# First MLP matrix on one Trainium2 core: upper and lower weight parts in fours, with a second copy of the input

## The chip, the cores and the metric

The program runs on one core of one Trainium2 chip. A core has TensorE (matrix products), VectorE, ScalarE, GpSimd and SyncE, which issues most of the transfers; in the profile they are PE (and PEld for its weight loads), DVE, ACT, POOL and SP. The metric is the device time of one execution in microseconds; lower is better. The kernel before takes 2034.71 us, the median of 3 runs (2034.69 to 2035.07).

## The reference

The reference is a small trunk of two layers over 256 tokens of width 2048 (all float32). Layer 0 mixes tokens with a convolution module, layer 1 with a latent attention; each is followed by an MLP with a squared ReLU. The MLP is what matters here:

```python
def sq_relu_mlp(h, w1, w2):
    return jnp.square(jax.nn.relu(h @ w1)) @ w2

# per layer: h is the RMS-normed input (256 x 2048),
# w1 is 2048 x 8192, w2 is 8192 x 2048
x = x + sq_relu_mlp(h, mlp_w1[layer], mlp_w2[layer])
```

## The kernel before

**Two parts per number.** The products keep float32 accuracy with a cheaper operand type (float32r). Every operand is split in an upper part, the value rounded to float32r, and a lower part, what is left. A product a x b is then three: upper x upper, upper x lower and lower x upper. ScalarE makes the upper part of the weights (`split_half`, L154, tile `hi`) and VectorE the lower part (L155, tile `lo`), from a raw tile that SyncE's queue loads from HBM (L144). There are three raw tiles, and six tiles each of `hi` and `lo`; one of these holds two k, a k being 128 rows of the weights.

**The input of the MLP.** The tokens are normed, transposed by TensorE (`to_T`, L237) and written as four tiles `xt`, each 128 x 4 x 512: for each k the upper part of 256 tokens (ScalarE, L186) and beside it the lower part of the same 256 tokens (VectorE, L193). `xhl(k)` is the whole 512 columns, `xh(k)` the first 256 alone. The transposes go through two PSUM buffers (`tr`). This happens block by block in `prepare`, while the product before (the last product of the convolution module or of the attention) still runs; the last block follows its end.

**The product with the first MLP matrix** (`mlp`, L397 and L398). The 8192 columns are taken in two halves of 8 groups of 512 columns. A group has four sums of 128 weight columns each, in four of the six PSUM buffers `acc`. For each of the 16 k, and each of the four sums, TensorE does two products. L397 takes the upper part of the weights as stationary operand and streams all 512 columns of `xhl(k)`; so upper x upper lands in the first half of the sum and upper x lower in the second half. L398 takes the lower part of the weights and streams the 256 columns of `xh(k)` into the first half. The order is L397, L398, L397, L398 and so on. At the end of a group ScalarE copies the second half out (L405), VectorE adds the first (L406), squares the positive part (L407), and both make the upper and lower parts `gh` and `gl` (L409, L410).

**The product with the second MLP matrix** (`product_A`, with `mm3` at L180 to L182) follows after each half. There `gh` and `gl` are stationary and the weights are streamed, 512 columns at a time, in the order `gh` x `hi`, `gl` x `hi`, `gh` x `lo`. `mm3` also serves the last products of the convolution module and of the attention, and the attention's input product, where `xt` is the stationary operand.

**What sets the order.** The convolution and attention stages have an order written out by hand. The MLP stages and the products around them are ordered by the framework's scheduler, which places instructions by its own costs; each engine then runs its list in order. Waits are semaphores between the lists.

**Where tiles lie.** Pools are stacked from both ends of the on-chip memory, and small pads (`PAD_CONST`, `PAD_SMALL`, `PAD_RIGHT`, `PAD_KV`, `PAD_O`) shift what follows. By the addresses of the built program `hi`, `lo`, `gh` and `gl` begin at multiples of 64 bytes, and `xt` begins 32 bytes off a multiple of 64. The first set of `xt` serves the convolution, the MLP of layer 0 and the attention's input; the second set is opened ahead of the MLP of layer 1.

Of the kernel before, what the change touches and what calls it, by code (L numbers as in the profile page):

```python
# [10 lines left out]
F32 = mybir.dt.float32  # L11
F32R = mybir.dt.float32r
# [6 lines left out]
P = 128  # L19
D = 2048  # L20
KC = D // P
T = 2
S = T * P
FF = 4 * D
NB = 512
NNB = D // NB
# [11 lines left out]
PAD_SMALL = 48  # L38
PAD_RIGHT = 48
PAD_KV = 40  # L40
PAD_O = 56
WB = 6
LOOK = WB // 2 - 1
# [29 lines left out]
def trunk_kernel(  # L73
# [26 lines left out]
    nc = tc.nc  # L100
# [8 lines left out]
    def repool(name, **banks):  # L109

        psum_cx[0].close()
        psum_cx[0] = ExitStack()
        for kind, n in banks.items():
            psum[kind] = psum_cx[0].enter_context(tc.tile_pool(name=kind + name, bufs=n, space=PSUM, reuse_waits="tile"))
# [13 lines left out]
    def nm(s):  # L128
        uid[0] += 1
        return f"{s}_{uid[0]}"  # L130
# [5 lines left out]
    def tr_tile():  # L136
        return psum["tr"].tile([P, NB], F32, tag="tr", name=nm("tr"))
# [46 lines left out]
    def hi_part(ps, hi, scale=1.0):  # L184

        nc.scalar.activation(hi, ps, AF.Copy, scale=scale)  # L186

    def lo_part(ps, hi, lo, scale=None):

        if scale is None:  # L190
            nc.vector.tensor_tensor(lo, ps, hi.bitcast(F32), op=ALU.subtract)
        else:
            nc.vector.scalar_tensor_tensor(  # L193
                out=lo, in0=ps, scalar=scale, in1=hi.bitcast(F32), op0=ALU.mult, op1=ALU.subtract
            )
# [33 lines left out]
            nc.vector.tensor_scalar(ms, ssq[:, :, 0], scalar1=1.0 / dim, scalar2=None, op0=ALU.mult)  # L229
        return rsqrt(ms, T, EPS, name)  # L230

    def to_T(src, k0, hi, lo, gain, pt=None):

        pt = pt if pt is not None else tr_tile()
        for j in range(2):
            for t in range(T):
                nc.tensor.transpose(  # L237
                    pt[:, j * S + t * P : j * S + (t + 1) * P],
                    src[:, t, (k0 + j) * P : (k0 + j + 1) * P],
                    ident,  # L240
                )
        ps = [pt[:, j * S : (j + 1) * S] for j in range(2)]
        for j in range(2):
            hi_part(ps[j], hi(k0 + j), gain[:, k0 + j : k0 + j + 1])
        for j in range(2):
            lo_part(ps[j], hi(k0 + j), lo(k0 + j), gain[:, k0 + j : k0 + j + 1])

    repool("c", acc=4, tr=2, sum=2)


    xs = main.tile([P, T, D], F32, name="xs")
# [31 lines left out]
    g_mlp = [vecs[:, 2 * KC : 3 * KC], vecs[:, 3 * KC : 4 * KC]]  # L283
# [1 line left out]
    b_dw = vecs[:, 6 * KC : 7 * KC]  # L285


    xt_cx, xt = [ExitStack()], []

    def right_pool(name, bufs):  # L290

# [3 lines left out]

    ctx.callback(lambda: xt_cx[0].close())

    def open_xt(name):
        pool = right_pool(name, 1)
        xt[:] = [  # L300
            pool.tile([P, KC // NNB, 2 * S], F32R, name=nm("xt")) for _ in range(NNB)
        ]

    xhl = lambda k: xt[k // 4][:, k % 4, :]
    xh = lambda k: xhl(k)[:, :S]
    xl = lambda k: xhl(k)[:, S:]
    open_xt("xt0")
    scratch = main.tile([P, NB], F32, name="scratch")

    xh_kt = lambda k, t: xh(k)[:, t * P : (t + 1) * P]  # L310
    xl_kt = lambda k, t: xl(k)[:, t * P : (t + 1) * P]

    def residual_stage(last, gain, r_scale=None):


        ssq = small.tile([P, T, NNB], F32, tag="ssq", name=nm("ssq")) if last else None

        def add(n, ps, t):
            sl = slice(n * NB, (n + 1) * NB)
            if r_scale is None:  # L320
                nc.vector.tensor_tensor(xs[:, t, sl], ps[t], xs[:, t, sl], op=ALU.add)
            else:
                nc.vector.scalar_tensor_tensor(
                    out=xs[:, t, sl], in0=ps[t], scalar=r_scale[:, t : t + 1], in1=xs[:, t, sl],
                    op0=ALU.mult, op1=ALU.add,
                )

        def prepare(n, only=None):
            sl = slice(n * NB, (n + 1) * NB)
            if last:  # L330
                if gain is not None:
                    for j in range(2):
                        to_T(xs, 4 * n + 2 * j, xh, xl, gain)
                for t in range(T) if only is None else [only]:
                    nc.scalar.activation(scratch, xs[:, t, sl], AF.Square, accum_out=ssq[:, t, n : n + 1])

        return ssq, add, prepare
# [39 lines left out]
    def mlp(layer, ssq, next_gain, finish=None):  # L377

        with ExitStack() as cx:
            mp = cx.enter_context(tc.tile_pool(name=f"mp{layer}", bufs=1, reuse_waits="tile"))  # L380
            nkh = FF // P // HALVES
            r2 = small.tile([P, T], F32, tag="r2", name=nm("r2"))
            nssq = None
            for hf in range(HALVES):
                hh, hl = [], []
                for g in range(nkh // 4):
                    ps = [acc_tile() for _ in range(4)]
                    c0 = (hf * nkh + 4 * g) * P
                    for u in range(KC // 4):
                        wj = load_split([rows(mlp_w1[layer], 4 * u, 4, c0, NB)], 4)  # L390
                        for j in range(4):
                            k = 4 * u + j
                            wh, wl = wj(j)
                            for b in range(4):
                                bs = slice(b * P, (b + 1) * P)

                                nc.tensor.matmul(ps[b], wh[:, bs], xhl(k), start=k == 0, stop=False)  # L397
                                nc.tensor.matmul(ps[b][:, :S], wl[:, bs], xh(k), start=False, stop=k == KC - 1)  # L398
                    gh = mp.tile([P, 4, S], F32R, tag="gh", name=nm("gh"), bufs=nkh // 4)
                    gl = mp.tile([P, 4, S], F32R, tag="gl", name=nm("gl"), bufs=nkh // 4)  # L400
                    for b2 in range(2):
                        v = mp.tile([P, 2, S], F32, tag="v", name=nm("v"), bufs=2)
                        for b in range(2):
                            o = ps[2 * b2 + b]
                            nc.scalar.activation(v[:, b, :], o[:, S:], AF.Copy)  # L405
                            nc.vector.tensor_tensor(v[:, b, :], o[:, :S], v[:, b, :], op=ALU.add)  # L406
                        nc.vector.scalar_tensor_tensor(out=v, in0=v, scalar=0.0, in1=v, op0=ALU.max, op1=ALU.mult)  # L407
                        bs = slice(2 * b2, 2 * b2 + 2)
                        nc.scalar.activation(gh[:, bs, :], v, AF.Copy)  # L409
                        nc.vector.tensor_tensor(gl[:, bs, :], v, gh[:, bs, :].bitcast(F32), op=ALU.subtract)  # L410
                    hh.append(gh)
                    hl.append(gl)
                if hf == 0:
                    r = rms_rstd(ssq, NNB, D, "n")
                    nc.vector.tensor_tensor(r2, r, r, op=ALU.mult)
                nssq, add, prepare = residual_stage(hf == HALVES - 1, next_gain, r2)
                product_A(
                    mlp_w2[layer],
                    hf * nkh,
                    nkh,  # L420
                    lambda k, t: hh[k // 4][:, k % 4, t * P : (t + 1) * P],
                    lambda k, t: hl[k // 4][:, k % 4, t * P : (t + 1) * P],
                    add,
                    prepare,
                    finish=(lambda t: finish(nssq, t)) if finish is not None and hf == HALVES - 1 else None,
                )
            return nssq


    with ExitStack() as cx:  # L430
# [172 lines left out]
        with tc.manual_schedule():  # L603
# [57 lines left out]
            for c in range(1, KC + 1):  # L661
                n = UC * c
# [81 lines left out]
            for m in range(NP):  # L744
# [4 lines left out]
                for j in range(2):  # L749
                    k = 2 * m + j  # L750
                    wh, wl = conv_w(NU + m, j)
                    for b in range(2):
                        bs = slice(b * NB, (b + 1) * NB)
# [2 lines left out]
                conv_split(NU + m + 2)  # L756
                conv_load(NU + m + 5)

        ssq, add, prepare = residual_stage(True, g_mlp[0])
        for b in range(2):  # L760
            for t in range(T):
                add(b, ps2[b], t)
# [58 lines left out]
    ssq = mlp(0, ssq, g_mix[1])  # L821


    with ExitStack() as cx:
# [98 lines left out]

        pad_kv = at.tile([P, PAD_KV], F32, name="pad_kv")
        nc.gpsimd.memset(pad_kv, 0.0)  # L925
# [4 lines left out]
        kpT = at.tile([P, S], F32, name="kpT")  # L930
        pad_o = at.tile([P, PAD_O], F32, name="pad_o")
        nc.gpsimd.memset(pad_o, 0.0)
# [168 lines left out]
        with tc.manual_schedule():  # L1101
# [8 lines left out]
            ps = [[acc_tile() for _ in range(2)] for _ in range(T)]  # L1110
            for k in range(KC):
                u, j = divmod(k, 2)
# [4 lines left out]
                wh, wl = w_at(("kv", u), j)  # L1117
# [9 lines left out]
            ps = [acc_tile() for _ in range(T)]  # L1127
            for k in range(KC):
                u, j = divmod(k, 4)
# [3 lines left out]
                wh, wl = w_at(("q", u), j)  # L1133
# [16 lines left out]
                if k == 13:  # L1150
                    pt = tr_tile()
# [31 lines left out]
            for g in range(NG):  # L1183
                for i in range(HG):
                    h = g * HG + i

                    n = -(-len(work) // (HG - i))
# [18 lines left out]
                o_piece(k)  # L1206
            prefetch()

        open_xt("xt1")
        ssq, add, prepare = residual_stage(True, g_mlp[1])  # L1210
        for b in range(2):
            for t in range(T):
                add(b, ps_o[b], t)
# [47 lines left out]
```

## Time and profile before

| | us |
|---|---|
| time, median of 3 runs | 2034.71 |
| the profiled execution's own time | 2034.44 |
| its span, first to last instruction | 2032.6 |
| TensorE busy | 2009.5 |
| VectorE busy | 1214.8 |
| ScalarE busy | 951.7 |
| GpSimd busy | 174.2 |
| granted TensorE clock, mean | 0.999 of full |
| memory traffic over the span | 180 GB/s |

In time order: the convolution module up to about 336 us, the first MLP (L397 first starts at 336.2), the attention between the MLPs, and the second MLP up to the end (L397 last starts at 1848.5; its second product follows).

How to read it: a row of the page's groups gives the line, the engine, the operation, output and inputs by tile names, the shape, the count, then busy time and the mean duration of one; the last column is the idle time of the engine ahead of them. The durations of TensorE's products overlap: a product's record includes the time until its last result is out, while the next one has already begun. So the distance between two starts, in the timeline, is the time that a product costs in a stream. Starts in the timeline are rounded to 0.01 us; a distance is therefore read over many products.

### The profile page before, as it was taken

What the parts mean: (1) busy time and instruction counts of PE and PEld (TensorE: products, weight loads), DVE (VectorE), ACT (ScalarE), POOL (GpSimd) and SP (SyncE); (2) the same over time, 40 slices, a digit from 0 to 9 for tenths busy, and PEclk for the clock granted to TensorE, in tenths of its full rate; (3) what the DMA queues carried; (4) which work ended last, traced back from release to release, by engine and by line L of the source; (5) the groups of instructions that cost most, each with busy time, mean ns of one, the idle gap of its engine ahead of it and who ended that gap; (6) DMA issues with size and microseconds to landing.
All of it is one profiled execution on the core that took longest, in us unless ns stands there. A gap on an engine that the chain in (4) does not pass through costs nothing.

```text
span 2032.6 us, 27882 instructions
## 1 busy us (share of the span) xinstructions
PE 2009.5 (99%) x11132; PEld 1747.1 (86%) x11132; DVE 1214.8 (60%) x1820; ACT 951.7 (47%) x1325; POOL 174.2 (9%) x101
## 2 busy tenths in 40 slices
PE   7999999999999999999999999999999999999998
PEld 7999888888888888888899887888888888888886
DVE  5999866665544465555446654665564455565454
ACT  5444655544433454444445444554443334454442
POOL 5887400000000000000000000000000000000000
PEclk9999999999999999999999999999999999999999
DMA  7555355665555665555555344566655566655552
GB/s 235 166 167 166 125 186 180 194 187 188 202 189 190 196 193 187 187 193 193 187 162 170 108 139 145 187 207 187 188 196 196 188 196 192 192 187 189 199 192 104
DMA packets 243268, 367.59 MB, mean 181 GB/s; under 512 B 15417, under 2 KB 89793, under 8 KB 242881
## 3 DMA queue, kind: packets, MB, share of 16 engines
q1 hardware_dynamic: 242400, 364.68, 56.0%
q8 instruction: 87, 1.43, 0.3%
q10 hardware_dynamic: 736, 1.12, 0.2%
q14 instruction: 45, 0.36, 0.0%
HBM read 363.68 MB, written 2.10 MB: 180 GB/s over the span
## 4 chain that ended last, share of the span: by engine, by line
PE 98%; DVE 1%; DMA 0%; ACT 0%; issue 0%; SPq 0%; DVEq 0%; ACTq 0%
PE acc L397 23%; PE acc L180 16%; PE acc L182 16%; PE acc L181 16%; PE acc L398 12%; PE acc L482 3%; PE acc L484 3%; PE acc L483 3%; PE sum L515 1%; PE acc L1049 1%; PE tr L237 1%; PE acc L1048 1%; PE acc L971 0%; PE acc L994 0%; PE acc L972 0%; PE acc L973 0%
## 5 line engine op out<-in xcount | busy, mean ns | idle before, releaser
L155 DVE TENSOR_TENSOR lo<-raw,hi 128x1024 fp32r<-128x1024 f32 (+1 forms) x628 | 755.2, 1206 | 685.1 <-ACT hi L154 673.3
L154 ACT ACTIVATE hi<-raw 128x1024 fp32r<-128x1024 f32 (+1 forms) x696 | 722.4, 1046 | 792.0 <-PE acc L181 458.3
L397 PE MATMUL acc<-xt,hi 128*128 128x512 f32 x2048 | 710.5, 390 | 0.0
L398 PE MATMUL acc<-xt,lo 128*128 128x256 f32 x2048 | 577.7, 282 | 0.0
L397 PEld LDWEIGHTS acc<-xt,hi 128*128 128x128 f32 x2048 | 384.4, 188 | 80.5
L180 PE MATMUL acc<-hi,gh 128*128 128x512 f32 x1024 | 398.6, 389 | 0.0
L182 PE MATMUL acc<-lo,gh 128*128 128x512 f32 x1024 | 398.4, 389 | 0.0
L181 PE MATMUL acc<-hi,gl 128*128 128x512 f32 x1024 | 398.4, 389 | 0.0
L398 PEld LDWEIGHTS acc<-xt,lo 128*128 128x128 f32 x2048 | 387.1, 189 | 0.1
L182 PEld LDWEIGHTS acc<-lo,gh 128*128 128x128 f32 x1024 | 192.2, 188 | 40.1
L180 PEld LDWEIGHTS acc<-hi,gh 128*128 128x128 f32 x1024 | 192.2, 188 | 39.7
L181 PEld LDWEIGHTS acc<-hi,gl 128*128 128x128 f32 x1024 | 192.2, 188 | 39.6
L549 DVE SCALAR_TENSOR_TENSOR sum<-ub,w_dw,sum 128x256 f32<-128x256 f32 x402 | 167.7, 485 | 4.9 <-ACT sum L518 2.9
L155 POOL TENSOR_TENSOR lo<-raw,hi 128x1024 fp32r<-128x1024 f32 x68 | 162.1, 2407 | 57.2 <-ACT hi L154 57.2
L482 PE MATMUL acc<-xt,hi 128*128 128x256 f32 x512 | 147.3, 288 | 0.0
L484 PE MATMUL acc<-xt,lo 128*128 128x256 f32 x512 | 143.2, 280 | 0.6 <-POOL lo L155 0.6
L483 PE MATMUL acc<-xt,hi 128*128 128x256 f32 x512 | 143.1, 279 | 0.0
L484 PEld LDWEIGHTS acc<-xt,lo 128*128 128x128 f32 x512 | 96.2, 188 | 0.8 <-POOL lo L155 0.8
L483 PEld LDWEIGHTS acc<-xt,hi 128*128 128x128 f32 x512 | 96.3, 188 | 0.6 <-DVE xt L193 0.2
L482 PEld LDWEIGHTS acc<-xt,hi 128*128 128x128 f32 x512 | 96.3, 188 | 0.4
L925 POOL MEMSET pad_kv<- 128x40 f32 x1 | 0.1, 132 | 772.6 <-PE acc L182 772.6
L405 ACT ACTIVATE v<-acc 128x256 f32<-128x256 f32 x128 | 46.4, 381 | 25.3 <-PE acc L398 25.3
(200 smaller groups left out, 1718.6 us busy)
## 6 DMA issues: line engine op xcount, KB each, us to landing
raw<-in_mlp_w SPq DMA_DIRECT2D x256, 1024.0 KB, 5.2
raw<-in_conv_w_pw SPq DMA_DIRECT2D x64, 512.0 KB, 4.9
raw<-in_conv_w_pw SPq DMA_DIRECT2D x16, 1024.0 KB, 5.1
raw<-in_mla_w_o SPq DMA_DIRECT2D x16, 1024.0 KB, 5.7
raw<-in_mla_w_kv_up SPq DMA_DIRECT2D x8, 1024.0 KB, 5.3
raw<-in_mla_w_in SPq DMA_DIRECT2D x8, 576.0 KB, 3.7
raw<-in_mla_w_in SPq DMA_DIRECT2D x4, 1024.0 KB, 5.0
raw<-in_mla_w_q_up SPq DMA_DIRECT2D x16, 256.0 KB, 3.2
```

What stands on the lines that cost most here:

```text
L154: nc.scalar.activation(hi, raw[:, js, :], AF.Copy)
L155: eng.tensor_tensor(lo, raw[:, js, :], hi.bitcast(F32), op=ALU.subtract)
L180: nc.tensor.matmul(ps, sh, mh, start=start, stop=False)
L181: nc.tensor.matmul(ps, sl, mh, start=False, stop=False)
L182: nc.tensor.matmul(ps, sh, ml, start=False, stop=stop)
L397: nc.tensor.matmul(ps[b], wh[:, bs], xhl(k), start=k == 0, stop=False)
L398: nc.tensor.matmul(ps[b][:, :S], wl[:, bs], xh(k), start=False, stop=k == KC - 1)
L405: nc.scalar.activation(v[:, b, :], o[:, S:], AF.Copy)
L482: nc.tensor.matmul(o, wh[:, bs], xh(k), start=k == 0, stop=False)
L483: nc.tensor.matmul(o, wh[:, bs], xl(k), start=False, stop=False)
L484: nc.tensor.matmul(o, wl[:, bs], xh(k), start=False, stop=k == KC - 1)
L549: nc.vector.scalar_tensor_tensor(out=out, in0=ubs[c][:, w : w + S], scalar=tap(c, w), in1=pcs[c], op0=ALU.mult, op1=ALU.add)
```

## The change

The four upper-part products of a k are done first, then the four lower-part products. The lower-part products no longer stream `xh(k)`, the first half of `xt`, but `xh2(k)`, a second copy of the upper part of the input in its own four tiles `xu` (128 x 4 x 256). ScalarE writes this copy from the same PSUM buffer as the first, behind the lower part, in `to_T`; 16 more activations for each MLP. A pad of 8 floats lies between `xt` and `xu`. The pool with both is opened ahead of each MLP's input, so the convolution's `xt0` keeps its place and layer 0's MLP gets a set of its own (`xt1`; layer 1's becomes `xt2`). By the addresses of the built program `xt1` and `xt2` begin at multiples of 64 bytes and `xu` begins 32 bytes off. The attention's input uses `xt1`, without a second copy. To make room, the scratch of the dynamic transfers at the bottom of the memory goes from 16,384 to 1,024 bytes, and all tiles above it on that side move down by 15,360 bytes.

```diff
+PAD_XT = 8
...
-    def to_T(src, k0, hi, lo, gain, pt=None):
+    def to_T(src, k0, hi, lo, gain, pt=None, hi2=None):
...
         for j in range(2):
             lo_part(ps[j], hi(k0 + j), lo(k0 + j), gain[:, k0 + j : k0 + j + 1])
+        for j in range(2 if hi2 is not None else 0):
+            hi_part(ps[j], hi2(k0 + j), gain[:, k0 + j : k0 + j + 1])
...
-    def open_xt(name):
+    def open_xt(name, twice=True):
         pool = right_pool(name, 1)
         xt[:] = [
             pool.tile([P, KC // NNB, 2 * S], F32R, name=nm("xt")) for _ in range(NNB)
         ]
+        if twice:
+            pad = pool.tile([P, PAD_XT], F32, name=nm("pad_xt"))
+            nc.gpsimd.memset(pad, 0.0)
+            xu[:] = [pool.tile([P, KC // NNB, S], F32R, name=nm("xu")) for _ in range(NNB)]
+
+    xh2 = lambda k: xu[k // 4][:, k % 4, :]
...
-    open_xt("xt0")
+    open_xt("xt0", False)
...
-                        to_T(xs, 4 * n + 2 * j, xh, xl, gain)
+                        to_T(xs, 4 * n + 2 * j, xh, xl, gain, hi2=xh2 if twice else None)
...
                                 nc.tensor.matmul(ps[b], wh[:, bs], xhl(k), start=k == 0, stop=False)
-                                nc.tensor.matmul(ps[b][:, :S], wl[:, bs], xh(k), start=False, stop=k == KC - 1)
+                            for b in range(4):
+                                bs = slice(b * P, (b + 1) * P)
+                                nc.tensor.matmul(ps[b][:, :S], wl[:, bs], xh2(k), start=False, stop=k == KC - 1)
...
-        ssq, add, prepare = residual_stage(True, g_mlp[0])
+        open_xt("xt1")
+        ssq, add, prepare = residual_stage(True, g_mlp[0], twice=True)
...
-        open_xt("xt1")
-        ssq, add, prepare = residual_stage(True, g_mlp[1])
+        open_xt("xt2")
+        ssq, add, prepare = residual_stage(True, g_mlp[1], twice=True)
...
-    nc = bacc.Bacc("TRN2", target_bir_lowering=False, num_devices=1)
+    nc = bacc.Bacc("TRN2", target_bir_lowering=False, num_devices=1, dynamic_dma_scratch_size=1024)
```

In the order that the scheduler made of the changed kernel, a new group of 512 columns begins with its first two sums alone, in twos of upper and twos of lower products, for fourteen products; then the third and fourth sums start and catch up. Before the change a group runs through its four sums from the first k on.

More of the change, by code (lines that the diff above doesn't have):

```diff
@@ L285, in trunk_kernel @@
     b_dw = vecs[:, 6 * KC : 7 * KC]
-    xt_cx, xt = [ExitStack()], []
+    xt_cx, xt, xu = [ExitStack()], [], []
     def right_pool(name, bufs):
@@ L311, in trunk_kernel, with residual_stage @@
     xl_kt = lambda k, t: xl(k)[:, t * P : (t + 1) * P]
-    def residual_stage(last, gain, r_scale=None):
+    def residual_stage(last, gain, r_scale=None, twice=False):
         ssq = small.tile([P, T, NNB], F32, tag="ssq", name=nm("ssq")) if last else None
```

## The prediction

> **What bounds the kernel now.** I read the page first: shares of the engines, then the chain that ended last, then the groups.
>
> ```profile
> PE 2009.5 (99%) x11132; PEld 1747.1 (86%) x11132; DVE 1214.8 (60%) x1820; ACT 951.7 (47%) x1325; POOL 174.2 (9%) x101
> PE 98%; DVE 1%; DMA 0%; ACT 0%; issue 0%; SPq 0%; DVEq 0%; ACTq 0%
> L397 PE MATMUL acc<-xt,hi 128*128 128x512 f32 x2048 | 710.5, 390 | 0.0
> L398 PE MATMUL acc<-xt,lo 128*128 128x256 f32 x2048 | 577.7, 282 | 0.0
> ```
>
> The chain is TensorE alone, and L397 and L398, the lines that the change rewrites, never waited (last column). So only the rate at which products follow each other counts. A "mean ns" includes a tail that overlaps the next product; the rate is the distance between two starts, and the timeline of TensorE shows it:
>
> ```profile
> 377.36 0.39 PE L397 MATMUL acc<-xt,hi 128*128 128x512 f32 x1
> ...
> 387.07 0.39 PE L397 MATMUL acc<-xt,hi 128*128 128x512 f32 x1
> ...
> 514.64 0.39 PE L180 MATMUL acc<-hi,gh 128*128 128x512 f32 x1
> 514.87 0.40 PE L181 MATMUL acc<-hi,gl 128*128 128x512 f32 x1
> 515.10 0.39 PE L182 MATMUL acc<-lo,gh 128*128 128x512 f32 x1
> 515.34 0.39 PE L180 MATMUL acc<-hi,gh 128*128 128x512 f32 x1
> 515.56 0.39 PE L181 MATMUL acc<-hi,gl 128*128 128x512 f32 x1
> ...
> 517.38 0.39 PE L180 MATMUL acc<-hi,gh 128*128 128x512 f32 x1
> ```
>
> Between the first two lines lie 28 pairs (one L397 and one L398): 9.71 us, **0.3468 us a pair**, 1.387 us for the four pairs of one k. At 514.64 the second product begins, a stream of 512-column products. Its first four take 0.92 us (514.64 to 515.56); from 515.34 on, nine take 2.04 us, **0.2267 each**. So such a stream needs three products to settle, at about 0.231. Streams of 256 columns, the same view elsewhere:
>
> ```profile
> 48.73 0.28 PE L483 MATMUL acc<-xt,hi 128*128 128x256 f32 x1
> ...
> 52.46 0.28 PE L482 MATMUL acc<-xt,hi 128*128 128x256 f32 x1
> ...
> 1090.33 0.39 PE L181 MATMUL acc<-hi,xt 128*128 128x512 f32 x1
> ...
> 1092.66 0.40 PE L182 MATMUL acc<-lo,xt 128*128 128x512 f32 x1
> 1092.89 0.28 PE L971 MATMUL acc<-kvh,hi 128*128 128x256 f32 x1
> ...
> 1093.36 0.28 PE L972 MATMUL acc<-kvl,hi 128*128 128x256 f32 x1
> ```
>
> From 48.73 to 52.46 there are 32 products: **0.1166 each**. The four that follow 512-column products at 1092.89 take 0.47 us, 0.1175 each. The ten before them take 2.33 us, 0.233 each, at the same 512 columns as the 0.2267. What differs is the place in memory: by the tiles' addresses, gh and the weights both begin at a multiple of 64 bytes, while xt begins 32 bytes off it. Before the change L397 and L398 stream an xt that is 32 bytes off against weights that are not. After it, the upper products stream an xt at a multiple of 64 (as the 0.2267 rows), the lower ones a copy that is 32 off (as the 0.1166 rows).
>
> **The change part by part.** The sum is made against the profiled execution, 2034.44 us (span 2032.6, 1.8 outside it), which lies 0.27 under the median 2034.71.
>
> *Order and addresses of the 4096 products.* There are 2 layers x 2 halves x 8 groups x 16 k = 512 fours. The four upper products of a k now follow four lower ones. The nearest row for their time is the stream that begins right behind L398: 0.92 us for four. The nearest for the four lower is the row behind 512-column products: 0.47. Sum 1.390 against 1.387, +0.003 x 512 = **+1.4 us**. Bounds: if both kinds run at their settled rates from the first product, 4 x 0.2267 + 4 x 0.1166 = 1.373, -0.014 x 512 = -7.2 us. If the upper ones run at 0.233 and the lower ones at 0.1201 (what a pair leaves beside a settled upper one, 0.3468 - 0.2267), 1.412, +12.7 us; I take neither, because the rows right behind a change of width exist and are nearest. Both ends are kept. In the built order about a sixth of the products come in twos, not fours (the first k of a group, below): the same rows hold, with more changes of width.
>
> *A rule that speaks against it.* Two rows alone give a fixed part and a part per column: with 0.2267 = 512p + c and 0.3468 = 768p + 2c, p is 0.416 ns and c 13.5 ns. If a product always costs c plus its columns, order and address cannot matter, and the sum of this step is 0. The row of 0.1166 stands 3.5 ns under what that gives for 256 columns (0.1201), so it does not hold fully.
> [...]
>
> *The same xt as stationary operand.* In the attention input, lines L180 to L182 load weights from xt: 96 products of 512 columns at 0.233 now, which get both operands at multiples of 64: 96 x 0.0063 = **-0.6 us**. The 192 of 288 columns run at 0.132 (26 in 3.43 us from 1060.05); no row shows them with equal addresses: between -1 and +1, taken as 0.
>
> *Copies.* Sixteen more ScalarE activations a layer, by the row of the first copy (128x256, 455/474/487 ns) 7.6 us a layer. They stand behind the lower parts, so they hold a transposing buffer longer; two buffers exist, and what waits for them is the transposes of the next block on TensorE. In the built order the third and fourth transposes stand 3 and 7 products later than before, 0.7 to 1.6 us, against two to four copies, 0.9 to 1.9 us. ScalarE waits 1.66 us ahead of each of its splits there, for TensorE to free buffers, so the copies are covered: 0. If the cover is gone, at most 1.9 us a layer, +3.8. Behind the copies in ScalarE's order stand the splits of weights, which are six buffers ahead.
>
> *Release of the sum buffers.* The four sums of a group now end within 0.35 us instead of 1.04, and there are six buffers for groups of four. Reading the first sum out takes 0.32 + 0.42 + 0.42 us from the start of its last product (ScalarE copy at 380.68 behind L398 at 380.36; VectorE add from 381.10 to 381.52), so it is free 0.7 us after the new group's start; the third upper product would be due at 0.45. That would be 0.3 to 0.4 us at 28 group boundaries, about +10. The built order hides it: the first two sums of a new group run through three k and more, fourteen products, some 2.4 us, before the third begins. Cost 0. The weights for that are six buffers ahead.
>
> *The rest at 0.* Two POOL memsets of the pad, one of 132 ns before; POOL is idle then. The DMA queue of SP has the same transfers in the same order, and ACT's DMA issues (positions, frequencies) come two copies later with nothing due. The smaller scratch moves all tiles by 15,360 bytes, 240 x 64, so distances below 64 stay. The new input tiles of the first MLP lie where the convolution's lay, whose last product started at 224.9 us; the first is written near 320. Waits added to TensorE: the first lower product of each k waits for the second copy, and behind it TensorE's whole queue would stand; but even the last block's copies, transposed during k = 0, are due twelve k or 16.6 us later.
>
> **Sum:** 2034.44 + 1.4 - 0.6 = 2035.2 by this execution, **2035.5 us** by the median.
>
> **The rivals.**
> - *Both streams settle at once* (for it: settled streams at both addresses hold their rates for hundreds of products; against: three slow products behind L398). -7.2 - 0.6: 2026.9 us. Chance 0.25, parts of the gain included.
> - *Nothing that tells apart*: the forecast, or the fixed cost per product, which gives 2034.1. Chance 0.40 together.
> - *The upper stream never settles*, because each run of four lower products throws it out again. Place: every k; price: uppers at 0.233, lowers at 0.1175, 1.402 a k, +7.7 - 0.6: 2041.8 us. It decides from 1.395 a k on, with lowers at 0.1175 uppers above 0.2313, hardly more than the 0.231 seen in the three unsettled products; this is why it is a close rival. For it: after a break at 1220.48 (attention output, same addresses) eight products take 1.85 us, 0.231. Chance 0.29.
> - *TensorE waits for the sums or the transposes after all*, +4 to +10 us. Against: the built order. Chance 0.06.
>
> **How the numbers follow.** 0.2% is 4.1 us, about what a measurement of this kernel can tell from no change. Faster 0.25, within 0.40, slower 0.35. For 8 in 10 I leave out the last of the gain (below 2028) and the ends of the slow cases (above 2042.5).
>
> **What the profile after would show.** Timeline in a group: fours of upper starts; 0.92 a four is my step, 0.907 the first rival, 0.93 the third. Lower fours 0.47 or 0.466. A k at 1.390. Idle time before the two lines stays 0.0; anything else there is the last rival, with its releaser named. L180 with xt at 512 columns falls to 0.227. The step that is weakest is the four upper products: no row shows a 512-column product behind a 256-column one whose own operand lies 32 bytes off in this order, beyond the four places where the second product begins.

## The result: 7.3 us slower, and the profile after

The changed kernel takes 2041.97 us (median of 6 runs, 2041.72 to 2042.48), the kernel before, on the same chip, 2034.70 (2034.55 to 2035.07). The ratio is 1.0036, with a 95% interval from 1.0026 to 1.0046: slower by 7.3 us, inside the range of the prediction, but above its 2035.5 and on the other side of its bound of 0.2%.

The page of the changed kernel, engines, chain and the groups of the two rewritten lines (L408 is the upper product, L411 the lower one; PEld is the weight load that runs ahead of each product; the columns after the bar are busy time, mean ns of one, and idle time ahead with what ended it):

```profile
PE 2016.9 (99%) x11132; PEld 1742.1 (85%) x11132; DVE 1214.0 (60%) x1820; ACT 951.8 (47%) x1357; POOL 174.2 (9%) x103
PE 97%; DVE 1%; SPq 1%; DMA 1%; ACT 0%; issue 0%; DVEq 0%; ACTq 0%
L408 PE MATMUL acc<-xt,hi 128*128 128x512 f32 x2048 | 574.4, 395 | 0.0
L408 PEld LDWEIGHTS acc<-xt,hi 128*128 128x128 f32 x2048 | 342.7, 188 | 43.4 <-DVE v L419 0.2
L411 PE MATMUL acc<-xu,lo 128*128 128x256 f32 x2048 | 337.8, 280 | 0.0
```

TensorE is still the bound, at the same share, and neither line shows idle time. One thing is new: a releaser stands behind the weight loads of L408, the VectorE adds of L419 that read the sums out. The busy times of L408 and L411 (574.4 and 337.8) can't be held against the 710.5 and 577.7 of before: overlapping products of one line are merged, and now four of a line stand together. The distances between starts must be read. TensorE's timeline in the middle of a group:

```profile
373.90 1.09 PE L408 MATMUL acc<-xt,hi 128*128 128x512 f32 x4
374.82 0.63 PE L411 MATMUL acc<-xu,lo 128*128 128x256 f32 x4
375.29 1.09 PE L408 MATMUL acc<-xt,hi 128*128 128x512 f32 x4
376.22 0.64 PE L411 MATMUL acc<-xu,lo 128*128 128x256 f32 x4
...
380.88 1.08 PE L408 MATMUL acc<-xt,hi 128*128 128x512 f32 x4
```

Four upper products take 0.92 to 0.93 us, four lower ones 0.47. From 373.90 to 380.88 lie five k: 6.98 us, 1.396 a k, against 1.387 before.

The page and the timeline round to 10 ns; the start times in the trace itself are in nanoseconds, and all rates below are means of distances between them, taken by the order of the products in the program. An "upper" distance runs from the start of an upper product to the next start, a stall is a distance above 245 ns (upper) or 130 ns (lower).

```
                                                before     after
four first-MLP stages, first to last start, us  178.35     180.24
                                                177.39     179.19
                                                178.35     180.18
                                                177.39     179.12
sum                                             711.50     718.74
mean upper distance without stalls, ns          228.35     231.73
mean lower distance without stalls, ns          118.33     117.47
stalls beyond those means, us                     0.42       2.50
first to last product less the four stages, us 1302.65    1302.80
```

Of the 7.5 us between the two profiled executions (2041.95 and 2034.44), 7.24 are inside the four stages. They are 2048 x (231.73 - 228.35) = +6.9 us of slower upper products, 2048 x (117.47 - 118.33) = -1.8 us of faster lower ones, and +2.1 us of stalls. The mean granted clock was 0.999 before and 0.998 after, and 1.00 in windows over the first and the third stage of both, so the clock is not the cause.

The stalls stand at the boundaries between groups of four sums. The timeline of all engines at one of them:

```profile
382.00 1.06 ACT L155 ACTIVATE hi<-raw 128x1024 fp32r<-128x1024 f32 x1 [1.73 <-PE acc L408]
382.27 0.63 PE L408 MATMUL acc<-xt,hi 128*128 128x512 f32 x2
382.97 1.18 ACT L418 ACTIVATE v<-acc 128x256 f32<-128x256 f32 x4
383.09 1.23 DVE L156 TENSOR_TENSOR lo<-raw,hi 128x1024 fp32r<-128x1024 f32 x1 [1.56 <-ACT hi L155]
...
384.24 1.08 DVE L419 TENSOR_TENSOR v<-acc,v 128x256 f32<-128x256 f32 x3
...
384.38 1.16 PE L408 MATMUL acc<-xt,hi 128*128 128x512 f32 x4
```

The new group begins at 382.27. ScalarE has a split of weights (L155) in hand until 383.06, so the copies of the old sums (L418) come 0.7 us late; then VectorE has its half of the split (L156) in hand until 384.32, so the adds (L419) come at 384.24. At 384.38 the third and fourth sum of the new group need the buffers that these adds free, and that run of four takes 1.16 us where the others take 1.08 or 1.09.

### The profile page after: what moved, and what is told of

Same layout as the page of the kernel before. It is cut to its first block, busy times and chain, and to the rows that moved or that the text cites. A ratio compares the mean times of both kernels' runs of the same rounds, so it can differ in the third digit from the quotient of the medians.

```text
span 2040.2 us, 27898 instructions
## 1 busy us (share of the span) xinstructions
PE 2016.9 (99%) x11132; PEld 1742.1 (85%) x11132; DVE 1214.0 (60%) x1820; ACT 951.8 (47%) x1357; POOL 174.2 (9%) x103
## 4 chain that ended last, share of the span: by engine, by line
PE 97%; DVE 1%; SPq 1%; DMA 1%; ACT 0%; issue 0%; DVEq 0%; ACTq 0%
PE acc L408 23%; PE acc L181 16%; PE acc L183 16%; PE acc L182 16%; PE acc L411 12%; PE acc L497 3%; PE acc L495 3%; PE acc L496 3%; PE sum L528 1%; PE acc L1063 1%; PE acc L1062 1%; PE tr L239 1%; PE acc L985 0%; PE acc L1008 0%; PE acc L987 0%; PE acc L986 0%
## 5 line engine op out<-in xcount | busy, mean ns | idle before, releaser
L156 DVE TENSOR_TENSOR lo<-raw,hi 128x1024 fp32r<-128x1024 f32 (+1 forms) x628 | 755.1, 1206 | 696.0 <-ACT hi L155 682.3
L155 ACT ACTIVATE hi<-raw 128x1024 fp32r<-128x1024 f32 (+1 forms) x696 | 721.8, 1045 | 780.6 <-PE acc L182 448.2
L408 PE MATMUL acc<-xt,hi 128*128 128x512 f32 x2048 | 574.4, 395 | 0.0
L408 PEld LDWEIGHTS acc<-xt,hi 128*128 128x128 f32 x2048 | 342.7, 188 | 43.4 <-DVE v L419 0.2
L411 PEld LDWEIGHTS acc<-xu,lo 128*128 128x128 f32 x2048 | 324.9, 188 | 50.0
L411 PE MATMUL acc<-xu,lo 128*128 128x256 f32 x2048 | 337.8, 280 | 0.0
L156 POOL TENSOR_TENSOR lo<-raw,hi 128x1024 fp32r<-128x1024 f32 x68 | 162.1, 2405 | 57.5 <-ACT hi L155 57.5
L497 PE MATMUL acc<-xt,lo 128*128 128x256 f32 x512 | 143.5, 280 | 0.6 <-POOL lo L156 0.6
L496 PEld LDWEIGHTS acc<-xt,hi 128*128 128x128 f32 x512 | 96.5, 188 | 0.6 <-DVE xt L194 0.2
L497 PEld LDWEIGHTS acc<-xt,lo 128*128 128x128 f32 x512 | 96.3, 188 | 0.8 <-POOL lo L156 0.8
L495 PEld LDWEIGHTS acc<-xt,hi 128*128 128x128 f32 x512 | 96.5, 188 | 0.4
L422 ACT ACTIVATE gh<-v 128x512 fp32r<-128x512 f32 x64 | 40.0, 624 | 50.4 <-DVE v L420 48.6
```

Of the source, the lines that this page charges most:

```text
L155: nc.scalar.activation(hi, raw[:, js, :], AF.Copy)
L156: eng.tensor_tensor(lo, raw[:, js, :], hi.bitcast(F32), op=ALU.subtract)
L411: nc.tensor.matmul(ps[b][:, :S], wl[:, bs], xh2(k), start=False, stop=k == KC - 1)
L495: nc.tensor.matmul(o, wh[:, bs], xh(k), start=k == 0, stop=False)
L496: nc.tensor.matmul(o, wh[:, bs], xl(k), start=False, stop=False)
L497: nc.tensor.matmul(o, wl[:, bs], xh(k), start=False, stop=k == KC - 1)
```

## Theories and experiments

The prediction left these open. **Theory A**: every change of width throws the stream of 512-column products out of its settled rhythm, and four are too few to find it again. **Theory B**: the new addresses are the cause, whatever the order. **Theory C**: products cost the same in any order, and the loss is waits for the sum buffers.

All results in one table. "Pair" is mean upper plus mean lower distance, without stalls; places are the offset of the moving operand within 64 bytes, upper and lower; the weights always lie at 0. Each ratio is to the kernel before on the same chip, 2034.7 to 2034.8 us.

```
run                       at a stretch  place   upper  lower  pair ns  stalls  time us   ratio [95%]
before                    1 (in turn)   32,32   228.4  118.3  346.7     0.4    2034.70   1
after                     4              0,32   231.7  117.5  349.2     2.5    2041.97   1.0036 [1.0026, 1.0046]
e1_order_alone            4             32,32   232.9  116.9  349.8     3.0    2043.73   1.0043 [1.0028, 1.0058]
e2_addresses_alone        1              0,32   231.0  118.3  349.3     0.4    2040.38   1.0027 [1.0018, 1.0037]
e4_last_k_in_pairs        4 (last k 1)   0,32   231.5  117.5  349.0     0.4    2039.70   1.0024 [1.0015, 1.0034]
e9_runs_16_by_sum         16             0,32   228.2  116.8  345.0     0.5    2031.31   0.9982 [0.9973, 0.9991]
e13_one_input_at_64       1              0,0    235.3  116.3  351.7     0.4    2046.74   1.0056 [1.0041, 1.0071]
e10_runs_16_old_place     16            32,32   233.3  116.7  350.0     0.4    2041.61   1.0034 [1.0021, 1.0046]
e14_runs_8                8              0,32   229.9  117.1  347.0     6.7    2041.86   1.0033 [1.0021, 1.0045]
e17_runs_32               32             0,32   227.4  116.7  344.2     0.5    2029.54   0.9973 [0.9962, 0.9984]
f1_runs_64                64             0,32   227.1  116.9  344.0    11.8    2040.35   1.0027 [1.0017, 1.0038]
f2_runs_8_staggered       8 and 16       0,32   228.9  116.9  345.8     0.4    2033.05   0.9991 [0.9982, 1.0000]
f3_fours_one_input        4              0,0    232.4  118.1  350.4     2.3    2044.68   1.0049 [1.0034, 1.0064]
f4_runs_32_one_input      32             0,0    227.5  119.8  347.3     0.5    2036.28   1.0007 [0.9998, 1.0017]
```

**The two halves of the change, each alone.** The order alone, in the kernel before:

```diff
+for b in range(4):
     nc.tensor.matmul(ps[b], wh[:, bs], xhl(k), start=k == 0, stop=False)
+for b in range(4):
     nc.tensor.matmul(ps[b][:, :S], wl[:, bs], xh(k), start=False, stop=k == KC - 1)
```

> The order of the change alone: four upper then four lower products, in the layout of before (no copy, the lower products read the same input as the upper ones, 32 bytes off a multiple of 64). Theory A (each change of width throws the 512-column stream out of its settled rhythm, and four products are too few to settle): uppers stay at 231 to 234 ns, lowers at 117 to 118, stalls at the group boundaries about 2 us, time 2040 to 2046 us. Theory B (the new addresses are the cause, the order is harmless): a k at 1.387 us as before, 2034.7 plus the boundary stalls of 2 us, 2035 to 2037. Theory C (products cost the same in any order and the loss is waits for the sum buffers): at 2048 pairs of 346.7 ns plus the waits, with waits of 2 us seen in the trace 2036.8.

Measured 2043.73 us; uppers 232.9, lowers 116.9, stalls 3.0 us. The time and the rates lie where theory A put them, and outside B and C. Theory A's reason doesn't hold here, though: sixteen at a stretch at these same addresses, below, settle at 233.3 and 116.7 ns, so these fours already run at the settled rates of their place. What the order alone costs is the 346.7 of the products in turn, not products that fail to settle. The addresses and the copies alone, in the changed kernel:

```diff
 for b in range(4):
     nc.tensor.matmul(ps[b], wh[:, bs], xhl(k), start=k == 0, stop=False)
-for b in range(4):
     nc.tensor.matmul(ps[b][:, :S], wl[:, bs], xh2(k), start=False, stop=k == KC - 1)
```

> The layout and the copies of the change alone: the input at a multiple of 64 bytes for the upper products, the copy 32 bytes off for the lower ones, but upper and lower products in turn as before. Theory A: a width change at every product, as before, so the pair has its own rhythm of 346.7 ns; copies hidden; 2034 to 2035.5 us, boundary stalls as before (0.4 us). Theory B: most of the 7.3 us stays: 2039 to 2042. Theory C: waits belong to the order, so 2034.7.

Measured 2040.38 us: theory A and C are wrong here, B is right. In turn from these addresses a pair takes 349.3 ns. So either half alone costs about as much as both together (+9.0, +5.6, and +7.3), and they do not add up. What both have in common is that they leave the one arrangement of before, products in turn with both inputs 32 bytes off, which holds 346.7 ns almost without a miss: in its trace the upper distances are 228 or 229 ns and the lower ones 118 or 119, all but 19 of 4092, and those 19 are among the first ten products of a stage. Outside the four stages the run with the addresses alone has 1302.67 us against 1302.65, and its stalls are those of before, so the sixteen copies a layer cost nothing.

**The stalls.** The changed kernel with its last k in pairs:

```diff
-for b in range(4): upper product of sum b
-for b in range(4): lower product of sum b
+if k == KC - 1:  for b in range(4): upper product of b, lower product of b
+else:            as it was
```

> The changed kernel, but the last k of each group of four sums has upper and lower products in turn, as before, so that the four sums end 0.35 us apart and not within 0.35 us. Theory A: the stalls at the 28 boundaries (2.1 us over those of before) go, the uppers of all other k stay at 231 to 232 ns: 2039 to 2040.5 us. Theory C: the whole loss goes with the waits: 2034.7 to 2035.5. Theory B: as A less the stalls, 2040.

Measured 2039.70 us, 2.3 less than the changed kernel; stalls 0.4 us as before. The idle column of its page (L410 is the upper product there) has lost its releaser:

```profile
L410 PEld LDWEIGHTS acc<-xt,hi 128*128 128x128 f32 x2048 | 350.9, 188 | 47.9
```

So 2.1 us of the loss are waits for the sum buffers, because the four sums end too close together; theory C explains no more than these. The other 5 stay with the rate of the products.

**Longer stretches.** Sixteen of a kind, sum by sum:

```diff
+for b in range(4):
+    for j in range(4):   # the four k of one tile of weights
         upper product of sum b, k = 4 * u + j
+for b in range(4):
+    for j in range(4):
         lower product of sum b, k = 4 * u + j
```

> The layout of the change, with sixteen upper products (four k of one tile of weights, sum by sum) and then sixteen lower ones at a stretch. Theory A: a change of width costs a fixed 13 to 20 ns over the settled products, paid four times more rarely: uppers 227.5 to 228.5 ns, lowers 116.6 to 117.5, sums end 0.47 us apart so the boundary stalls go as well; 128 stretches of 5.51 to 5.53 us against 5.55 before, 2029 to 2032.5 us, faster than both kernels. Theory B: the length of a stretch does not matter, 2040 to 2042. Theory C: only the waits go, 2034 to 2036.

Measured 2031.31 us, theory A's range, faster than both kernels. TensorE's timeline in it (L406 upper, L410 lower):

```profile
375.80 3.81 PE L406 MATMUL acc<-xt,hi 128*128 128x512 f32 x16
379.45 2.03 PE L410 MATMUL acc<-xu,lo 128*128 128x256 f32 x16
381.32 3.81 PE L406 MATMUL acc<-xt,hi 128*128 128x512 f32 x16
```

Sixteen uppers take 3.65 us, 0.228 each, sixteen lowers 1.87, 0.117. Mean distance by place in the stretch, in ns:

```
place   1      2      3      4      5      6      7      8     ...  16
upper   229.9  235.6  228.4  232.4  230.7  226.6  226.6  226.8 ...  226.6
lower   119.2  116.7  116.6  116.7  116.8  116.6  116.7  116.8 ...  116.7
```

This shows why fours can't reach the settled rates of the new addresses. An upper stream behind lower products needs five products to settle; their excess over 226.7 is 3.2 + 8.9 + 1.7 + 5.7 + 4.0 = 23.5 ns, and the first lower one costs 2.5 more: 26 ns for one change each way. The first four uppers average 231.6, and the changed kernel, whose stretches end there, has 231.7. Only the mean agrees: place by place its fours take 232.1, 232.9, 231.7 and 229.1.

If the cost goes by the number of changes, stretches of eight and thirty-two can be worked out from this. Eight:

```diff
 as the run of sixteen, with
-for j in range(4)
+for j0 in (0, 2): uppers of k = 4u + j0, 4u + j0 + 1; then their lowers
```

> The layout of the change, eight upper and eight lower products at a stretch (two k, sum by sum). Theory A, by the run of sixteen: the first five uppers behind a change of width cost 24 ns over the settled 226.7 in all, the first lower 2.5; the uppers of a stretch of eight average 229.6 to 230.5, the lowers 117, and with some stretches of four to six at the group boundaries the time is 2034 to 2036.5 us. If the cost did not go by the number of changes of width, the time would stay at the 2031.3 of the run of sixteen or go to the 2039.7 of the fours.

Measured 2041.86 us, which fits neither expectation. The rates are as expected, 229.9 and 117.1, but 6.7 us of stalls came on top, as the idle column of its page and a boundary in its timeline show:

```profile
L406 PEld LDWEIGHTS acc<-xt,hi 128*128 128x128 f32 x2048 | 362.8, 188 | 71.7 <-DVE v L418 10.7
```

```profile
382.34 1.23 DVE L156 TENSOR_TENSOR lo<-raw,hi 128x1024 fp32r<-128x1024 f32 x1 [1.55 <-ACT hi L155]
...
383.38 1.77 PE L406 MATMUL acc<-xt,hi 128*128 128x512 f32 x6
383.49 1.08 DVE L418 TENSOR_TENSOR v<-acc,v 128x256 f32<-128x256 f32 x3
...
383.95 0.77 PEld L406 LDWEIGHTS acc<-xt,hi 128*128 128x128 f32 x4 [0.38 <-DVE v L418]
```

It is the mechanism of the changed kernel's boundary at a higher price: the add that frees the third sum stands behind VectorE's half of a split, and TensorE's loads wait 0.38 us for it. To separate rate from wait, eight in the two middle tiles of a group and sixteen in its first and last, so that the sums end 0.47 us apart:

```diff
+m = 4 if u in (0, KC // 4 - 1) else 2
-for j0 in (0, 2): ...
+for j0 in range(0, 4, m): ...
```

> Eight of a kind at a stretch in the two middle tiles of a group, sixteen in its first and last tile, so that the four sums end 0.47 us apart as in the run of sixteen. Theory A (the 2041.9 of the run of eight was 6.3 us of waits for sum buffers, and the rest a change of width at 26.5 ns): two more changes of width for each of the 32 groups than in the run of sixteen, 64 at 26.5 ns, 1.7 us: 2032.6 to 2033.5 us. Rival: stretches of eight are slow in themselves: 2036 us and up, with rates of upper products over 231 ns.

Measured 2033.05 us, 1.74 above the run of sixteen, where 64 x 26.5 ns make 1.70; stalls 0.4 us. Thirty-two:

```diff
-for u in range(KC // 4):          # one tile of weights
+for u in range(0, KC // 4, 2):    # two tiles, j over eight k
```

> The layout of the change, thirty-two products of a kind at a stretch: eight k, two tiles of weights. Theory A: half as many changes of width as in the run of sixteen, 64 fewer at 26.5 ns, so 1.7 us less: 2029.3 to 2030 us. Rival: four of the six half tiles of split weights are held by one stretch, so the splits of the next tiles come late and the two lines show idle time; each boundary of a stretch would then lose 0.2 us or more, 2035 us and up.

Measured 2029.54 us, 1.77 below the run of sixteen, again 64 changes at 26.5. Its timeline (L406 upper, L410 lower):

```profile
381.84 7.44 PE L406 MATMUL acc<-xt,hi 128*128 128x512 f32 x32
389.12 3.90 PE L410 MATMUL acc<-xu,lo 128*128 128x256 f32 x32
392.85 3.36 PE L406 MATMUL acc<-xt,hi 128*128 128x512 f32 x14
```

7.28 us for 32 uppers, 0.2275 each, and 3.73 for 32 lowers, 0.1166. It is the best kernel of this study, 5.2 us under the kernel before and 12.4 under the changed one. Sixty-four, by turning the order round in the second half of each group:

```diff
+for upper in (True, False) if u == 0 else (False, True):
+    the thirty-two products of that kind
```

> As the run of thirty-two, and every second stretch of eight k takes the lower products first, so that 64 of a kind follow each other. Theory A: 32 changes of width fewer each way than in the run of thirty-two, at 26.5 ns, 0.8 us less: 2028.4 to 2029 us. Rival: the splits of weights come late; then the lines show idle time and it is 2030 us or more.

Measured 2040.35 us: the rival. The settled rates are the best of all (227.1 and 116.9), but 11.3 us of stalls stand before the lower products. The idle column of its page, and the place in its timeline (L410 is the lower product):

```profile
L410 PE MATMUL acc<-xu,lo 128*128 128x256 f32 x2048 | 254.9, 282 | 1.0 <-DVE lo L156 1.0
```

```profile
389.89 3.09 ACT L155 ACTIVATE hi<-raw 128x1024 fp32r<-128x1024 f32 x3
390.03 7.98 PE L410 MATMUL acc<-xu,lo 128*128 128x256 f32 x64
...
393.32 4.64 DVE L156 TENSOR_TENSOR lo<-raw,hi 128x1024 fp32r<-128x1024 f32 x4 [4.32 <-ACT hi L155]
394.60 3.20 PEld L410 LDWEIGHTS acc<-xu,lo 128*128 128x128 f32 x26 [0.18 <-DVE lo L156]
```

VectorE makes the next lower part from 393.32 on, one in 1.2 us. The row names ScalarE, but ScalarE had written the upper part for it by 389.98, 3.3 us earlier. By the times VectorE waits for a buffer of `lo`: the first half tile of this stretch is read last by a lower product that starts at 392.95. The second half of the lower products walks through four half tiles for its first sum alone, eight products, 0.9 us; at 394.60 its loads have waited 0.18 us for a lower part. Six buffers of split weights are enough for thirty-two at a stretch, not for sixty-four.

**The addresses.** Sixteen at a stretch in the layout of before, without a copy:

```diff
 as the run of sixteen, in the kernel before; the lower products read
-xh2(k)
+xh(k)
```

> Sixteen upper and sixteen lower products at a stretch as in the run of sixteen, but in the layout of before: one input, 32 bytes off, no copy. Theory A (what costs is the change of width; once settled the address does not matter): uppers 227.5 to 229 ns, lowers 116.6 to 117.2, time 2030 to 2033 us. Theory B3 (the settled rate of 512 columns hangs on the offset, as the rows with a stationary operand 32 bytes off show, 233): uppers 232 to 234 ns, lowers 116.7 to 117, time 2038 to 2042 us.

Measured 2041.61 us. Theory A fell in its strict form (once settled, the address does not matter); the rival B3 is right. Timeline (L395 upper, L399 lower):

```profile
376.33 3.90 PE L395 MATMUL acc<-xt,hi 128*128 128x512 f32 x16
380.07 2.03 PE L399 MATMUL acc<-xt,lo 128*128 128x256 f32 x16
381.93 3.90 PE L395 MATMUL acc<-xt,hi 128*128 128x512 f32 x16
```

Sixteen uppers from an input 32 bytes off take 3.74 us (0.2333 each in the mean of all), and no place of the stretch gets faster (231.5 to 234.8 in the means); the lowers 1.86, as from the copy. A pair takes 350.0 ns in sixteens and 349.8 in fours at these addresses, so the 26 ns for a change of width belong to the new addresses, not to every stream. Thirty-two at a stretch, the lower products from the input at a multiple of 64:

```diff
-nc.tensor.matmul(ps[b][:, :S], wj(j)[1][:, bs], xh2(k), ...
+nc.tensor.matmul(ps[b][:, :S], wj(j)[1][:, bs], xh(k), ...
```

> The run of thirty-two with the lower products reading the same input as the upper ones, at a multiple of 64 bytes (the copies are read by nobody). If settled lower products run at 116.7 ns from either offset, the copy is not needed: 2029 to 2030 us. If the settled rate hangs on the offset, as that of 512 columns does (226.7 at a multiple of 64, 233.3 at 32 off), the lowers average 118 to 120 ns and the time is 2032 to 2037 us.

Measured 2036.28 us, lowers 119.8: here too the settled rate changes with the place, the other way round. So the best settled rates are 226.7 for 512 columns from a multiple of 64 and 116.7 for 256 columns from 32 off; the other offsets give 233.3 and 119.8. The change puts both inputs at the better places, and without the copy the run of thirty-two would lose 6.7 us. The same exchange in fours:

```diff
-nc.tensor.matmul(ps[b][:, :S], wl[:, bs], xh2(k), ...
+nc.tensor.matmul(ps[b][:, :S], wl[:, bs], xh(k), ...
```

> The changed kernel with its fours, its layout and its copies, but the lower products read the same input as the upper ones, at a multiple of 64 bytes (the copies are read by nobody). If the offset of the copy helps as it did in turn (349.3 ns a pair with the copy, 351.7 without): 2046 to 2048 us. If the offset of the lower products does not matter in fours: 2041.5 to 2042.5 us.

Measured 2044.68 us, between the two expectations: the copy's offset is worth 2.7 us in fours, 0.6 ns on each lower and 0.65 on each upper product. And in turn, one input at a multiple of 64 for both:

```diff
-nc.tensor.matmul(ps[b][:, :S], wl[:, bs], xh2(k), ...   # in turn
+nc.tensor.matmul(ps[b][:, :S], wl[:, bs], xh(k), ...    # in turn
```

> Upper and lower products in turn, as before, and the lower ones read the same input as the upper ones, as before; only that input lies at a multiple of 64 bytes (the copies are still written, and read by nobody). Theory A2 (a pair in turn is locked at 346.7 ns where both products stream from the same offset within 64 bytes, and thrown out of step where the offsets differ): pair 346.7, time 2034 to 2035.5 us. Theory B2 (512 columns from a multiple of 64 next to 256-column products are slow in themselves): pair 349 to 350, time 2039.5 to 2041.5 us.

Measured 2046.74 us (2044.66 to 2048.68). Both theories fell: equal offsets do not give the 346.7 ns, and the time is above B2's. In the trace the first stage runs at one rate and the other three at another. Upper products of the first and of the second stage, thirty pairs apart in each (L408 is the upper product):

```profile
399.89 0.40 PE L408 MATMUL acc<-xt,hi 128*128 128x512 f32 x1
...
410.29 0.40 PE L408 MATMUL acc<-xt,hi 128*128 128x512 f32 x1
...
749.86 0.40 PE L408 MATMUL acc<-xt,hi 128*128 128x512 f32 x1
...
760.46 0.40 PE L408 MATMUL acc<-xt,hi 128*128 128x512 f32 x1
```

10.40 us in the first stage, 346.7 ns a pair; 10.60 in the second, 353.3. The two lines and their inputs' addresses are the same.

## Why the prediction was right in its range and wrong in its likeliest case

- **The bound: right.** TensorE alone, at 99%, and only the distances between starts count. The loss is where the change is.
- **Four uppers and four lowers, 1.390 us a k: wrong by 7 ns.** This step failed. Lowers 0.47 were right (4 x 117.5). Uppers were put at 0.92, by the one row of a stream right behind L398; they take 4 x 231.7 = 0.927. That gives 1.397 a k, past the 1.395 from which the prediction let its third rival decide. The term is (349.20 - 346.68) x 2048 = +5.2 us instead of +1.4. "A stream needs three products to settle" was read rightly in its row and carried to a place where it doesn't hold. Rounding was not the mistake: in the trace's nanoseconds that row is 231, 232, 231, 227, 921 in all, and the three other places where a second product begins give 920 or 921. But there the stream follows the products in turn, one lower product after each upper one, and its operands are others; behind sixteen lower products the first four take 926 ns and the stream needs five to settle. The changed kernel's fours take 926 too, its twos at the start of a group 932 for four, which makes the mean 927. The prediction itself named this step its weakest.
- **The rival that happened** is "the upper stream never settles", priced at 2041.8 with chance 0.29. For the rates at the new addresses its mechanism is shown by the distances at each place of a longer stretch and by the staggered run, the run of sixteen and that of thirty-two, which differ by 26 to 28 ns a change. It isn't the whole reason why the kernel is slower than before: the order alone loses more, with products that are settled. Its price was partly luck: it took 0.233 for the uppers (measured 0.2317) and had no stalls.
- **Release of the sum buffers, costed at 0: wrong, +2.1 us.** The cover was counted rightly, some 2.4 us before the third sum. The other side was too short: 0.7 us to free the first sum, from a boundary of before where ScalarE and VectorE came to the sums at once. After the change the sums end while both have a split of weights in hand, and the first add starts 2.0 us after the new group. The rival with waits was put at +4 to +10 where the cover is gone; the run of eight shows that price, 6.3 us more than before.
- **Both streams settle at once, 2026.9: wrong for fours**, but the rates it used, 0.2267 and 0.1166, are the settled ones of the long stretches.
- **Nothing that tells apart: wrong.** By a fixed 13.5 ns a product and 0.416 ns a column, order and address change nothing. The runs disagree: the same 512 columns take 226.7 to 235.3 ns in the means, by address and by what went before, while the page gives a weight load of the upper product 188 or 189 ns in every run.
- **The same xt as stationary operand, -0.6 us: half right.** The 96 products of 512 columns went from 22.61 to 22.19 us in all, the 192 of 288 columns from 25.61 to 25.82: -0.2 us.
- **Copies at 0 and the rest at 0: right**, shown by the run with the addresses alone.

Sum with the measured terms: 5.2 + 2.1 - 0.2 = +7.1, against 7.3 measured.

## What to carry to other kernels

Where TensorE is the bound, time a stream by the distance between starts, at every place behind a change of width, before choosing how many products stand together: from the new addresses a change cost 26 ns, so fours lost and thirty-twos won with the same copy; from the old ones it cost nothing that could be seen. An arrangement can hold a good rhythm that its parts don't have alone, as the products in turn did, and here either half of the change lost it; so do each half of a change alone. When sums are made to end together, look at what the engines that read them out have in hand at that moment, and let the sums end one after the other.

## What the runs showed that was not expected

- The settled rate of a product changes with where its moving operand lies, and in opposite ways for the two widths: 512 columns 226.7 ns from a multiple of 64, 233.3 from 32 off; 256 columns 119.8 and 116.7. No other offset was run, and no run moved the offset alone: the tile's whole address, and for 256 columns its row length, changed with it. The rows before have 512 columns at 0.233 where the moving weights lie at a multiple of 64 and the stationary `xt` 32 off, so it may be the two operands' places against each other that count.
- A stream of alternating widths can fall into a cycle and keep it for a stage. Consecutive distances in the second stage of the run with one input at a multiple of 64 (upper, lower, ...), in ns:

```
233 117 241 120 236 113 | 233 117 241 120 236 113 | 233 117 241 120 ...
```

  Three pairs make 1060 ns, 353.3 a pair. The first stage of the same run went by another cycle, of 346.7, to its end, with the same two lines and the same addresses of the inputs. What differs is the moment at which the stage began, and eight transposes among the first products of the first and the third stage; the third is slow all the same. The four times of this kernel also spread over 4.0 us, some of which such cycles would explain (one stage in the other cycle is 512 x 6.7 ns = 3.4 us). That the moment of entry chooses the cycle is argued, not shown, and what in the chip makes these cycles stays open.
- The pair in turn with both inputs 32 bytes off (346.7) is faster than the settled rates of the same two addresses together (233.3 + 116.7 = 350.0): alternation helped the kernel before.
